# A fused transformer block: softplus on VectorE, the scan's operands in four tiles of their own, its temporaries in the residual's tiles

## The chip, the core and the metric

The kernel runs on one core of a Trainium2 chip. The metric is device microseconds of one execution, the median over runs. TensorE (PE) is shown in two rows of the profile, PE for matmuls and PEld for weight loads; VectorE is DVE, ScalarE is ACT, GpSimd is POOL, and SP is the queue that issues all DMAs. Instructions of an engine run in the order in which they stand in its program, and an instruction that waits holds up everything behind it on that engine.

## What is computed

Two transformer blocks follow each other on 512 tokens of width 1024. The change lies in the first, in the state-space branch beside the banded attention. Per token and head a step size is made from a narrow projection; it scales a causal decay, and a chunked scan (four chunks of 128 tokens here, two groups of eight heads) carries a state from chunk to chunk:

```python
dt = jax.nn.softplus(dt_raw + dt_bias)
A = -jnp.exp(a_log)
X = x * dt[..., None];  a = dt * A
decay_in = jnp.exp(where(tril, a_cum[l] - a_cum[s], -inf))
y_diag = (C B^T * decay_in) X          # per chunk
states = B^T (exp(a_cum[-1] - a_cum) * X)
y_off  = C prev * exp(a_cum)           # prev: state carried so far
h = h + concat(att, gated ssd) @ w_out
```

The residual `h` is first needed where the output projection of the first block is added to it.

## The kernel before

All dense products run as three fp32r matmuls each (high and low halves, lines 167 to 175), in units of 24 matmuls of 128x512 for each 512 KB of weights. A unit is loaded by SP (line 137), its high half is made by ACT (line 156, tile wh) and its low half by DVE or POOL (line 157, tile wl). Three raw buffers and two of each half rotate; the split of a unit runs one unit ahead of its use.

The order of the matmuls on PE is the order of the code. The other engines' instructions are placed by a scheduler that works from its own timeline, by priority; inside `tc.high_priority()` an instruction is placed before others that could run. The dense stream is a generator that yields after every 12 matmuls; such a stretch is called a tick here. `drive` (line 221) lets the side work advance at each tick: a `yield True` of a side generator ends its turn for that tick, so what follows it in the code comes at least one tick of dense matmuls later on PE. In the first dense stage (`dense1`, lines 794 to 798) one side moves per tick, in the second (`dense1z`) two.

The side work that matters:

- `norm_side` (466): sums of squares for the first norm. In line 472 it also starts the eight loads of the residual, 256 KB each, into the tiles `h`, which until then held the transposed input; SP issues them in the first 30 us, and nothing reads them before the output projection.
- `conv` (481): of each finished row of 128 channels a depthwise convolution: line 483 takes the row out of PSUM into `u`, ACT scales it (485), three DVE steps add the shifted copies (487), ACT takes a tanh (490), DVE finishes (491). It runs on every unit of the first dense stage, so DVE is busy with it while the step size is made.
- `dt_side` (496): the narrow projection, then the softplus as a series. Lines 511 to 521 are on DVE and ACT, lines 522 to 533 are 21 instructions on POOL, on tiles of 128x64 (one of 128x16), each waiting for the one before. The last ones make `da` (the decay exponent, line 531) and its high and low parts `dah` and `dal`. Eight ticks later PE sums `da` over the tokens (lines 537 to 539), ACT takes the exponential `ex` (540).
- `am_pair` (565): for half the heads of one scan step, ACT writes eight 128x128 blocks, the lower-triangle mask scaled by `dah` and `dal`, into two tiles. They come from the shared arena RA, of which 16 tiles are free then, so ACT can write them several steps ahead.
- `ssd_side` (573): the scan, eight steps, first the four chunks of group 0, then those of group 1. At the head of a step PE makes C B^T (591) and the segment sums of both halves (604, 605; they read the four `am` tiles), ACT takes the exponentials (608), DVE multiplies by the masked C B^T (609). One tick later (two in the first two steps) PE multiplies the result with X (622, 16 small matmuls), the carried state (629) and makes the new state (636). X, Xd, M and t are temporaries of the arena FA.
- `val_evac` (651): at the end of the last unit of `dense1`, ACT takes four banks of values out of PSUM (line 654). The next dense matmul (the first row of q) goes to the first of these banks.

Temporaries, attention and gating share FA, 28 tiles.

Of the kernel before, what the change touches and what calls it, by code (L numbers as in the profile page):

```python
# [9 lines left out]
F32 = mybir.dt.float32  # L10
F32R = mybir.dt.float32r
I32 = mybir.dt.int32
AF = mybir.ActivationFunctionType
ALU = mybir.AluOpType
# [59 lines left out]
class Both:  # L74
# [11 lines left out]
    def room(self, n):  # L86
        return len(self.own.free_list) + len(self.shared.free_list) >= n


@with_exitstack  # L90
def mixer_kernel(ctx, tc, xT, xN, wst, wfa, wfb, wdt, wgrp, rbt, par, con, frow, out):
# [313 lines left out]
    with ExitStack() as ph:  # L405
# [4 lines left out]
        RB = Both(Arena(fa_p, 5, F32R, "fx"), RA)  # L410
        lw = {}
# [54 lines left out]
        def norm_side():  # L466
            for _ in range(4):
                yield True
            ssb = col_sums(acc)
            FA.put(acc)  # L470
            for k in range(KD):
                nc.sync.dma_start(out=h[k], in_=xN[(k // 2) * 128:(k // 2 + 1) * 128, (k % 2) * 512:(k % 2 + 1) * 512])
            rsqrt(rcol1, ssb[:, 0:NT], NT, 1.0 / D, 1e-5)
            V.tensor_scalar(out=rhalf1, in0=rcol1, scalar1=0.5, scalar2=None, op0=ALU.mult)
            dg = bcast_diag(rcol1, FA)
            yield True
            yield True
            lw["rb1"] = bcast_rows(dg, FA)
            yield True
# [16 lines left out]
        def dt_side():  # L496
# [12 lines left out]
            with tc.high_priority():  # L509
# [12 lines left out]
                G.tensor_tensor(out=dz, in0=dz, in1=du, op=ALU.mult)  # L522
                G.tensor_tensor(out=dz2, in0=dz, in1=dz, op=ALU.mult)
                G.tensor_scalar(out=dp, in0=dz2, scalar1=2.0 / 15, scalar2=2.0 / 13, op0=ALU.mult, op1=ALU.add)
                for n in (11, 9, 7, 5, 3, 1):
                    G.tensor_tensor(out=dp, in0=dp, in1=dz2, op=ALU.mult)
                    G.tensor_scalar(out=dp, in0=dp, scalar1=2.0 / n, scalar2=1.0, op0=ALU.add, op1=ALU.mult)
                G.tensor_tensor(out=dp, in0=dp, in1=dz, op=ALU.mult)
                G.tensor_tensor(out=dt, in0=dx, in1=dp, op=ALU.add)
                G.tensor_scalar(out=aexp, in0=aexp, scalar1=-1.0, scalar2=1.0, op0=ALU.mult, op1=ALU.mult)  # L530
                G.tensor_tensor(out=v3(da), in0=v3(dt), in1=bc_mid(aexp, NT), op=ALU.mult)
                G.tensor_copy(out=dah, in_=da)
                G.tensor_tensor(out=dal, in0=da, in1=dah.bitcast(F32), op=ALU.subtract)
# [29 lines left out]
        prev = {}  # L563

        def am_pair(c, g, q):
            o = c * 16 + g * 8 + q * 4
            amh, aml = RA.take(2)
            for t, a in ((amh, dah.bitcast(F32)), (aml, dal)):
                for j in range(4):
                    S.activation(out=col(t, j), in_=C("le"), func=AF.Copy, scale=a[:, o + j:o + j + 1])  # L570
            return amh, aml

        def ssd_side():
# [3 lines left out]
            am = [am_pair(0, 0, 0), am_pair(0, 0, 1)]  # L577
            yield False
            for n, (c, g) in enumerate(seq):
# [8 lines left out]
                X = FA.get()  # L588
# [7 lines left out]
                if c < NT - 1:  # L596
                    Xd = FA.get()
# [4 lines left out]
                for q in range(2):  # L602
# [3 lines left out]
                    RA.put(*am[q])  # L606
                    M = FA.get()
# [3 lines left out]
                if n + 1 < len(seq):  # L611
                    c1, g1 = seq[n + 1]
                    am = [am_pair(c1, g1, 0), am_pair(c1, g1, 1)]
                G.tensor_tensor(out=h8(xt), in0=h8(xt), in1=bc_in(P("d_skip")[:, g * 8:g * 8 + 8], 64), op=ALU.mult)
                yield True
                if n < 2:
                    yield True
# [6 lines left out]
                FA.put(*Ms)  # L624
                FA.put(X)
                V.tensor_tensor(out=xt, in0=xt, in1=yb, op=ALU.add)
                if c > 0:
                    ob = ax_bank()
                    PE.matmul(ob, lhsT=col(CT, c), rhs=prev[g], start=True, stop=True)
                    t = FA.get()  # L630
                    V.tensor_tensor(out=h8(t), in0=h8(ob), in1=hs(ex[:, 0:64], c, g), op=ALU.mult)
                    G.tensor_tensor(out=xt, in0=xt, in1=t, op=ALU.add)
                    FA.put(t)
                if c < NT - 1:
                    nb = ax_bank()
                    PE.matmul(nb, lhsT=bt, rhs=Xd, start=True, stop=True)
                    FA.put(Xd)
# [9 lines left out]
                yield True  # L647

# [112 lines left out]
        def z_evac(g):  # L761
            def f(c, b):
                y = xs_tok[c, g]
# [738 lines left out]
```

## Time and profile before

| what | value |
|---|---|
| time, median of 3 runs | 1442.28 us (1441.97 to 1442.55) |
| the profiled execution | 1444.04 us, of it 1442.3 us of span, 1.7 us around it |
| mean granted TensorE clock | 0.998 |
| busy: PE, DVE, ACT, POOL | 1421.2, 1006.5, 695.8, 235.7 us |
| the change's stage | about 40 to 240 us of the span |

How to read the profile's rows: a row of the timeline has the start in us, the time in us, engine, line, operation, tiles (out<-in) and a count where several are merged; in square brackets stands how long the engine was idle before it and what ended the wait. Rows of several instructions overlap at the ends, because an instruction's start can lie before the end of the one ahead: what an instruction costs its engine is the distance from its start to the next start. Rows of the windows give, for each stretch, the busy time of each engine, then the granted clock (PEclk, 1.00 is full speed).

### The profile page before, as it was taken

How to read it: one execution, taken by the hardware profiler on the slowest of the kernel's cores; microseconds unless marked ns; L12 is line 12 of the kernel's file. 1: busy time of each engine (PE TensorE's matmuls, PEld its weight loads, DVE VectorE, ACT ScalarE, POOL GpSimd, SP SyncE). 2: the span in 40 equal slices, each digit the busy share in tenths (PEclk: the TensorE clock that was granted, in tenths of full speed). 3: DMA queues.
4: the chain of work that ended last, by engine and by line, in shares of the span. 5: the costliest groups of instructions: out<-in, count | busy, mean ns of one | idle time of the engine just before them, and what ended most of it. 6: DMA issues, size and time to landing. Idle time of an engine off the chain costs nothing.

```text
span 1442.3 us, 18031 instructions
## 1 busy us (share of the span) xinstructions
PE 1421.2 (99%) x6683; PEld 1172.9 (81%) x6683; DVE 1006.5 (70%) x1763; ACT 695.8 (48%) x1236; POOL 235.7 (16%) x220
## 2 busy tenths in 40 slices
PE   8999999999999999999999999999999999999998
PEld 5777888888888888888878888888888888888887
DVE  7774565655977778677774666777645977878676
ACT  5584645424544435345444646464324544545453
POOL 4322520000010010102262433221110010010101
PEclk9999999999999999999999999999999999999999
DMA  7221532223533241420233433342233433141411
GB/s 256 60 87 54 138 98 81 71 88 112 180 96 114 65 149 44 161 74 30 95 92 96 125 95 99 103 116 68 88 102 126 167 103 117 59 146 45 161 30 59
DMA packets 46408, 145.91 MB, mean 101 GB/s; under 512 B 5872, under 2 KB 6128, under 8 KB 46320
## 3 DMA queue, kind: packets, MB, share of 16 engines
q1 hardware_dynamic: 46320, 144.76, 32.4%
q8 instruction: 52, 0.85, 0.3%
q14 instruction: 36, 0.29, 0.1%
HBM read 131.63 MB, written 2.10 MB: 93 GB/s over the span
## 4 chain that ended last, share of the span: by engine, by line
PE 83%; DVE 9%; POOL 2%; ACT 2%; issue 2%; DMA 1%; SPq 0%; POOLq 0%; ACTq 0%; DVEq 0%
PE mm L170 13%; PE mm L168 13%; PE mm L169 13%; PE mm L173 10%; PE mm L174 10%; PE mm L175 10%; DVE wl L157 2%; PE ax L174 2%; PE ax L173 2%; PE ax L175 2%; DVE s L1258 1%; PE ax L728 1%; PE ax L1270 1%; PE ax L384 1%; PE ax L622 1%
## 5 line engine op out<-in xcount | busy, mean ns | idle before, releaser
L168 PE MATMUL mm<-r,wh 128*128 128x512 f32 x928 | 368.2, 397 | 3.0 <-ACT wh L156 2.9
L170 PE MATMUL mm<-r,wl 128*128 128x512 f32 x928 | 362.4, 391 | 1.5 <-DVE wl L157 1.5
L169 PE MATMUL mm<-r,wh 128*128 128x512 f32 x928 | 362.3, 390 | 1.4 <-DVE r L294 1.0
L156 ACT ACTIVATE wh<-wr 128x1024 fp32r<-128x1024 f32 (+1 forms) x173 | 182.4, 1054 | 369.3 <-PE mm L169 151.0
L157 DVE TENSOR_TENSOR wl<-wr,wh 128x1024 fp32r<-128x1024 f32 (+1 forms) x171 | 230.3, 1347 | 118.0 <-ACT wh L156 117.4
L168 PEld LDWEIGHTS mm<-r,wh 128*128 128x128 f32 x928 | 174.7, 188 | 40.8 <-ACT wh L156 3.3
L169 PEld LDWEIGHTS mm<-r,wh 128*128 128x128 f32 x928 | 174.6, 188 | 39.3 <-DVE r L294 2.0
L173 PE MATMUL mm<-wh,r 128*128 128x512 f32 x512 | 206.3, 403 | 0.0
L170 PEld LDWEIGHTS mm<-r,wl 128*128 128x128 f32 x928 | 174.6, 188 | 39.0 <-DVE wl L157 2.5
L174 PE MATMUL mm<-wl,r 128*128 128x512 f32 x512 | 199.7, 390 | 0.3 <-DVE wl L157 0.3
L175 PE MATMUL mm<-wh,r 128*128 128x512 f32 x512 | 199.8, 390 | 0.0
L299 POOL TENSOR_TENSOR vl<-u,vh 128x512 fp32r<-128x512 f32 x36 | 48.2, 1350 | 751.0 <-ACT vh L298 682.7
L174 PEld LDWEIGHTS mm<-wl,r 128*128 128x128 f32 x512 | 96.4, 188 | 21.6 <-issue 2.2
L173 PEld LDWEIGHTS mm<-wh,r 128*128 128x128 f32 x512 | 96.4, 188 | 21.2 <-issue 2.2
L175 PEld LDWEIGHTS mm<-wh,r 128*128 128x128 f32 x512 | 96.1, 188 | 20.4
L298 ACT ACTIVATE vh<-u 128x512 fp32r<-128x512 f32 x100 | 63.0, 631 | 50.7 <-PE mm L175 36.5
L938 DVE TENSOR_TENSOR h<-h,mm 128x512 f32<-128x512 f32 x80 | 52.4, 679 | 19.7 <-PE mm L175 19.7
L353 ACT ACTIVATE s<-s,nm 128x128 f32<-128x128 f32 (+1 forms) x96 | 52.6, 550 | 19.1 <-DVE nm L350 19.1
L298 ACT ACTIVATE wh<-u 128x1024 fp32r<-128x1024 f32 (+1 forms) x32 | 32.3, 1009 | 61.2 <-PE mm L175 61.2
L298 ACT ACTIVATE wh<-t 128x1024 fp32r<-128x1024 f32 x32 | 34.0, 1063 | 56.1 <-PE mm L169 32.5
L299 DVE TENSOR_TENSOR wl<-u,wh 128x1024 fp32r<-128x1024 f32 (+1 forms) x32 | 38.0, 1188 | 24.7 <-ACT wh L298 24.7
L299 DVE TENSOR_TENSOR vl<-u,vh 128x512 fp32r<-128x512 f32 x64 | 43.7, 682 | 0.0
(342 smaller groups left out, 2335.2 us busy)
## 6 DMA issues: line engine op xcount, KB each, us to landing
wr<-in_wst_dram SPq DMA_DIRECT2D x171, 512.0 KB, 3.6
u<-in_wfa_dram SPq DMA_DIRECT2D x32, 512.0 KB, 4.6
u<-in_wfb_dram SPq DMA_DIRECT2D x32, 512.0 KB, 4.4
r<-r SPq DMA_DIRECT2D x56, 128.0 KB, 2.8
h<-in_xT_dram SPq DMA_DIRECT2D x8, 256.0 KB, 6.3
h<-in_xN_dram SPq DMA_DIRECT2D x8, 256.0 KB, 4.7
f<-in_rbt_dram SPq DMA_DIRECT2D x8, 256.0 KB, 2.9
gr<-gr SPq DMA_DIRECT2D x16, 128.0 KB, 2.7
```

Of the source, the lines that this page charges most:

```text
L156: S.activation(out=hi[:, p], in_=t[:, p], func=AF.Copy)
L157: eng.tensor_tensor(out=lo[:, p], in0=t[:, p], in1=hi.bitcast(F32)[:, p], op=ALU.subtract)
L168: PE.matmul(ps, lhsT=wh, rhs=xh, start=first, stop=False)
L169: PE.matmul(ps, lhsT=wh, rhs=xl, start=False, stop=False)
L170: PE.matmul(ps, lhsT=wl, rhs=xh, start=False, stop=last)
L173: PE.matmul(ps, lhsT=xh, rhs=wh, start=first, stop=False, **kw)
L174: PE.matmul(ps, lhsT=xh, rhs=wl, start=False, stop=False, **kw)
L175: PE.matmul(ps, lhsT=xl, rhs=wh, start=False, stop=last, **kw)
L298: S.activation(out=hi, in_=src, func=AF.Copy)
L299: (eng or V).tensor_tensor(out=lo, in0=src, in1=hi.bitcast(F32), op=ALU.subtract)
L353: S.activation(out=s[:, SOFF[i]:SOFF[i] + n], in_=s[:, SOFF[i]:SOFF[i] + n], func=AF.Exp, bias=nm[:, i:i + 1], accum_out=Z[:, i:i + 1])
L938: V.tensor_tensor(out=ht(c, g), in0=ht(c, g), in1=b, op=ALU.add)
```

## The change

Five things are done, in the first block alone.

1. The softplus series moves from POOL to DVE: the 21 instructions there become 15 on DVE, since the multiply by the square and the addition of the next coefficient now go in one step. They stay inside `tc.high_priority()`.
2. `am_pair` takes its tiles from a new arena AM of four tiles. Four is what one scan step holds, so the tiles of the next step are written only after PE has read those of the present one.
3. The scan's steps are spread: the two halves of the next step's operands are written on two ticks, so that each step has two ticks between its head and its products with X (before: two in the first two steps, one in the others), and the first step starts one tick later.
4. X, Xd, M and t live in the eight tiles `h`. The loads of the residual move from `norm_side` to the end of `ssd_side`.
5. An assertion at the gate's evacuation, without an instruction.

```diff
+class Loan(Arena):
+    def __init__(self, tiles):
+        self.free_list = list(tiles)
+        self.low = len(tiles)
...
+        AM = Arena(fa_p, 4, F32R, "fm")
...
-            for k in range(KD):
-                nc.sync.dma_start(out=h[k], in_=xN[(k // 2) * 128:(k // 2 + 1) * 128, (k % 2) * 512:(k % 2 + 1) * 512])
             rsqrt(rcol1, ssb[:, 0:NT], NT, 1.0 / D, 1e-5)
...
-                G.tensor_tensor(out=dz, in0=dz, in1=du, op=ALU.mult)
-                G.tensor_tensor(out=dz2, in0=dz, in1=dz, op=ALU.mult)
-                G.tensor_scalar(out=dp, in0=dz2, scalar1=2.0 / 15, scalar2=2.0 / 13, op0=ALU.mult, op1=ALU.add)
-                for n in (11, 9, 7, 5, 3, 1):
-                    G.tensor_tensor(out=dp, in0=dp, in1=dz2, op=ALU.mult)
-                    G.tensor_scalar(out=dp, in0=dp, scalar1=2.0 / n, scalar2=1.0, op0=ALU.add, op1=ALU.mult)
-                G.tensor_tensor(out=dp, in0=dp, in1=dz, op=ALU.mult)
-                G.tensor_tensor(out=dt, in0=dx, in1=dp, op=ALU.add)
-                G.tensor_scalar(out=aexp, in0=aexp, scalar1=-1.0, scalar2=1.0, op0=ALU.mult, op1=ALU.mult)
-                G.tensor_tensor(out=v3(da), in0=v3(dt), in1=bc_mid(aexp, NT), op=ALU.mult)
-                G.tensor_copy(out=dah, in_=da)
-                G.tensor_tensor(out=dal, in0=da, in1=dah.bitcast(F32), op=ALU.subtract)
+                V.tensor_tensor(out=dz, in0=dz, in1=du, op=ALU.mult)
+                V.tensor_tensor(out=dz2, in0=dz, in1=dz, op=ALU.mult)
+                V.tensor_scalar(out=dp, in0=dz2, scalar1=2.0 / 15, scalar2=None, op0=ALU.mult)
+                for n in (13, 11, 9, 7, 5, 3):
+                    V.scalar_tensor_tensor(out=dp, in0=dp, scalar=2.0 / n, in1=dz2, op0=ALU.add, op1=ALU.mult)
+                V.scalar_tensor_tensor(out=dp, in0=dp, scalar=2.0, in1=dz, op0=ALU.add, op1=ALU.mult)
+                V.tensor_tensor(out=dt, in0=dx, in1=dp, op=ALU.add)
+                V.tensor_scalar(out=aexp, in0=aexp, scalar1=-1.0, scalar2=None, op0=ALU.mult)
+                V.tensor_tensor(out=v3(da), in0=v3(dt), in1=bc_mid(aexp, NT), op=ALU.mult)
+                V.tensor_copy(out=dah, in_=da)
+                V.tensor_tensor(out=dal, in0=da, in1=dah.bitcast(F32), op=ALU.subtract)
...
+        FB = Loan(h)
 
         def am_pair(c, g, q):
             o = c * 16 + g * 8 + q * 4
-            amh, aml = RA.take(2)
+            amh, aml = AM.take(2)
...
-            am = [am_pair(0, 0, 0), am_pair(0, 0, 1)]
-            yield False
+            am = []
+            for q in range(2):
+                am.append(am_pair(0, 0, q))
+                yield True
...
-                X = FA.get()
+                X = FB.get()
...
-                    RA.put(*am[q])
-                    M = FA.get()
+                    AM.put(*am[q])
+                    M = FB.get()
...
-                if n + 1 < len(seq):
-                    c1, g1 = seq[n + 1]
-                    am = [am_pair(c1, g1, 0), am_pair(c1, g1, 1)]
                 G.tensor_tensor(out=h8(xt), in0=h8(xt), in1=bc_in(P("d_skip")[:, g * 8:g * 8 + 8], 64), op=ALU.mult)
-                yield True
-                if n < 2:
+                am = []
+                for q in range(2):
+                    if n + 1 < len(seq):
+                        am.append(am_pair(*seq[n + 1], q))
                     yield True
                 yb = ax_bank()
...
                 yield True
+            for k in range(KD):
+                nc.sync.dma_start(out=h[k], in_=xN[(k // 2) * 128:(k // 2 + 1) * 128, (k % 2) * 512:(k % 2 + 1) * 512])
```

The line numbers of the changed kernel are higher by 4 to 8 in this part: 483, 487, 491 become 488, 492, 496; 531 becomes 535; 541 becomes 545; 570 becomes 575; 608 becomes 615; 622 becomes 628; 654 becomes 662.

The scheduler places the instructions of DVE and ACT anew. On DVE, before, this stood where the last pieces of the convolution of row 3 (tile f_164) are added up; the series is on POOL, and the only trace of it here is `dtdo` (dt is its result, ex the exponential of the sums):

```order
L541 TENSOR_TENSOR dtdo<-dt,ex 128x64
L487 SCALAR_TENSOR_TENSOR f_164<-u_260,cw,f_164 128x512
L157 TENSOR_TENSOR wl<-wr,wh 128x1024
L483 TENSOR_TENSOR u_260<-mm,rb 128x512
L487 SCALAR_TENSOR_TENSOR f_166<-u_259,cw,f_166 128x512 x3
L491 SCALAR_TENSOR_TENSOR f_164<-f_165,f_164 128x512
```

Now the end of the series stands there, the rest of it one by one between the convolution's steps ahead of this place (dp is the series' value, dz_254 the square):

```order
L492 SCALAR_TENSOR_TENSOR f_164<-u_264,cw,f_164 128x512
L531 SCALAR_TENSOR_TENSOR dp<-dp,dz_254 128x64
L532 SCALAR_TENSOR_TENSOR dp<-dp,dz 128x64
L533 TENSOR_TENSOR dt<-dx,dp 128x64
L496 SCALAR_TENSOR_TENSOR f_164<-f_165,f_164 128x512
L535 TENSOR_TENSOR da<-dt,aexp 128x64
L536 CAST dah<-da 128x64
L537 TENSOR_TENSOR dal<-da,dah 128x64
L545 TENSOR_TENSOR dtdo<-dt,ex 128x64
```

So `da` now comes behind the last step of the convolution of row 3, which itself waits for ACT's tanh f_165. Ahead of this place, from the moment PE has finished row 3 (u_264 is read out of PSUM), DVE has in this order: line 488, 492, 496, one step of the series, the low half of a unit (line 163), 492 twice, a step of the series, 492, 496, a step of the series, and then the rows shown.

On ACT, in the third scan step (chunk 2 of group 0), before, this was the end of the step's work: the second exponential (line 608), the rest of the operands two steps later (tiles r_118, r_119), and then the four values (line 654):

```order
L608 ACTIVATE f_160<-ax 128x512
L570 ACTIVATE r_118<-con,dah 128x128 x2
L570 ACTIVATE r_119<-con,dal 128x128 x4
L654 ACTIVATE f_164<-mm,rcol_127 128x512
L654 ACTIVATE f_156<-mm,rcol_127 128x512
L654 ACTIVATE f_157<-mm,rcol_127 128x512
L654 ACTIVATE f_152<-mm,rcol_127 128x512
```

Now the same instructions stand in nearly the same order (fm_175 and fm_176 are the third and fourth of the four tiles):

```order
L615 ACTIVATE h_89<-ax 128x512
L575 ACTIVATE fm_175<-con,dah 128x128 x2
L575 ACTIVATE fm_176<-con,dal 128x128 x2
L662 ACTIVATE f_154<-mm,rcol_127 128x512
L575 ACTIVATE fm_176<-con,dal 128x128
L662 ACTIVATE f_156<-mm,rcol_127 128x512
```

What moved is not visible on ACT but on PE: this scan step's head now stands one tick later there, 12 matmuls before the end of the last value unit; before, it stood 24 ahead of it.

On SP the eight loads of the residual now stand, four and four, around one weight load, behind the last scan step, which in PE's order comes after 636 dense matmuls (the last scan step came after 552 before); the output projection begins after 768.

More of the change, by code (lines that the diff above doesn't have):

```diff
@@ L596, in ssd_side @@
                 if c < NT - 1:
-                    Xd = FA.get()
+                    Xd = FB.get()
                     G.tensor_tensor(out=h8(Xd), in0=h8(xt), in1=hs(dtdo, c, g), op=ALU.mult)
@@ L623, in ssd_side @@
                                   start=True, stop=True)
-                FA.put(*Ms)
-                FA.put(X)
+                FB.put(*Ms)
+                FB.put(X)
                 V.tensor_tensor(out=xt, in0=xt, in1=yb, op=ALU.add)
@@ L629, in ssd_side @@
                     PE.matmul(ob, lhsT=col(CT, c), rhs=prev[g], start=True, stop=True)
-                    t = FA.get()
+                    t = FB.get()
                     V.tensor_tensor(out=h8(t), in0=h8(ob), in1=hs(ex[:, 0:64], c, g), op=ALU.mult)
                     G.tensor_tensor(out=xt, in0=xt, in1=t, op=ALU.add)
-                    FA.put(t)
+                    FB.put(t)
                 if c < NT - 1:
@@ L636, in ssd_side @@
                     PE.matmul(nb, lhsT=bt, rhs=Xd, start=True, stop=True)
-                    FA.put(Xd)
+                    FB.put(Xd)
                     if c == 0:
@@ L762, in f @@
             def f(c, b):
+                assert ("ssd", g) in ready
                 y = xs_tok[c, g]
```

## The prediction

> **What bounds the kernel now.** I read the page first, then PE's timeline for its gaps, then what ended each gap.
>
> ```profile
> span 1442.3 us, 18031 instructions
> PE 1421.2 (99%) x6683; PEld 1172.9 (81%) x6683; DVE 1006.5 (70%) x1763; ACT 695.8 (48%) x1236; POOL 235.7 (16%) x220
> ```
>
> PE is busy for all but 21 us, and the change takes no matmul away. So it can only win gaps of PE, and the time that the clock is lowered behind a gap. PE's timeline in the change's stage (each row with the gap ahead of it):
>
> ```profile
> 63.17 0.33 PE L537 MATMUL ax<-da,con 128*128 128x64 f32 x2
> ...
> 66.13 0.39 PE L169 MATMUL mm<-r,wh 128*128 128x512 f32 x1
> 66.36 0.39 PE L170 MATMUL mm<-r,wl 128*128 128x512 f32 x1
> 69.62 0.50 PE L168 MATMUL mm<-r,wh 128*128 128x512 f32 x1 [2.88 <-ACT wh L156]
> ...
> 70.88 0.79 PE L170 MATMUL mm<-r,wl 128*128 128x512 f32 x1 [0.38 <-DVE wl L157]
> ```
> ```profile
> 91.62 0.50 PE L604 MATMUL ax<-r,gt_r 128*128 128x512 f32 x1 [0.79 <-ACT f L555]
> ...
> 100.42 1.67 PE L622 MATMUL ax<-f,f 128*128 128x64 f32 x8 [1.79 <-DVE f L609]
> ```
> ```profile
> 119.70 0.38 PE L591 MATMUL ax<-f,f 128*128 128x128 f32 x2
> ...
> 119.95 0.48 PE L604 MATMUL ax<-r,gt_r 128*128 128x512 f32 x1
> ...
> 120.97 0.39 PE L173 MATMUL mm<-wh,r 128*128 128x512 f32 x1
> ...
> 123.70 1.00 PE L622 MATMUL ax<-f,f 128*128 128x64 f32 x8
> 125.84 1.10 PE L622 MATMUL ax<-f,f 128*128 128x64 f32 x8 [1.14 <-DVE f L609]
> ```
>
> A dense matmul costs 66.36 - 66.13 = 0.23 us, a tick of twelve 123.70 - 120.97 = 2.73 us. Five gaps lie here. The first comes from the softplus: ACT's operands for the scan (line 570) stand in ACT's program ahead of a unit's high half (line 156), and they wait for POOL's series.
>
> ```profile
> 62.15 2.16 ACT L570 ACTIVATE r<-con,dah 128x128 fp32r<-128x128 f32 x7 [4.88 <-POOL dah L532]
> ...
> 68.53 1.04 ACT L156 ACTIVATE wh<-wr 128x1024 fp32r<-128x1024 f32 x1
> ```
> ```profile
> 49.70 0.58 POOL L522 TENSOR_TENSOR dz<-dz,du 128x64 f32<-128x64 f32 x1 [23.30 <-DVE dz L521]
> ...
> 61.15 0.33 POOL L531 TENSOR_TENSOR da<-dt,aexp 128x64 f32<-128x64 f32 x1
> 61.53 0.58 POOL L532 CAST dah<-da 128x64 fp32r<-128x64 f32 x1
> ```
>
> POOL takes from 49.70 to 61.48 for `da`. PE wants it at 63.17 and has it; only ACT is late. The granted clock shows what a gap costs behind itself:
>
> ```profile
> 70.00:74.00 4.00, 3.62 (x10) 2.53 (x9) 4.00 (x7) 4.00 (x13) 0.00 (x0) 0.57 0.43 131
> 100.00:104.00 4.00, 3.58 (x11) 2.55 (x12) 2.77 (x5) 1.86 (x5) 0.00 (x0) 0.60 0.00 0
> 124.00:128.00 4.00, 2.86 (x18) 2.13 (x17) 1.48 (x3) 2.81 (x9) 0.06 (x1) 1.00 0.28 112
> ```
>
> Behind the gap of 2.88 us the clock is 0.57 over 4 us, behind that of 1.79 it is 0.60, behind 1.14 it stays at 1.00. A lowered stretch loses up to 0.43 x 4 = 1.7 and 0.40 x 4 = 1.6 us.
>
> **The change part by part.**
>
> *What goes, 10.4 us.* With the operands written step by step, no operand waits ahead of the high half any more: the gap at 69.62 goes (69.62 - 66.36 - 0.23 = 3.0 us), the one at 70.88 (0.4) and the clock behind them (1.7): 5.1 us. With two ticks between a step's head and its products everywhere and with the scan one tick later, the gaps at 91.62 (0.8), 100.42 (1.8 and 1.6 of clock) and 125.84 (1.1) go: 5.3 us. What is late next there: the second half of M. In the old third step the second exponential starts at 124.48, 4.8 us behind the step's head at 119.70, and M is done 1.4 us later (125.84); with two ticks PE wants it at 1.27 + 2 x 2.73 + 0.45 = 7.2 us. One us of cover is left, so I put these at nothing.
>
> *The series on DVE, 7.5 us of new loss.* DVE's rows give the price of each kind of step between starts:
>
> ```profile
> 43.30 0.22 DVE L514 TENSOR_TENSOR dx<-dx,dz 128x64 f32<-128x64 f32 x1
> 43.43 1.41 DVE L487 SCALAR_TENSOR_TENSOR f<-u,cw,f 128x512 f32<-128x512 f32 x2
> 44.76 0.22 DVE L515 TENSOR_TENSOR dx<-dx,par 128x64 f32<-128x64 f32 x1
> 45.24 1.23 DVE L157 TENSOR_TENSOR wl<-wr,wh 128x1024 fp32r<-128x1024 f32 x1 [0.26 <-ACT wh L156]
> 46.38 1.41 DVE L487 SCALAR_TENSOR_TENSOR f<-u,cw,f 128x512 f32<-128x512 f32 x2
> ...
> 47.81 0.69 DVE L483 TENSOR_TENSOR u<-mm,rb 128x512 f32<-128x512 f32 x1
> 48.41 0.68 DVE L491 SCALAR_TENSOR_TENSOR f<-f,f 128x512 f32<-128x512 f32 x1
> 49.01 0.55 DVE L521 RECIPROCAL dz<-dz 128x64 f32<-128x64 f32 x1
> ...
> 60.64 0.69 DVE L483 TENSOR_TENSOR u<-mm,rb 128x512 f32<-128x512 f32 x1 [0.49 <-PE mm L170]
> ```
>
> A small step costs 43.43 - 43.30 = 0.13 us, or its whole 0.22 when the next one needs it; a convolution step 0.66 (44.76 - 43.43, halved), a low half 1.14, lines 483 and 491 0.60 each. In the series the arithmetic is short: 15 x 0.2 = 3 us against POOL's 12. But DVE's program puts the convolution between its steps. The row at 60.64 waits for PE alone, so it stands there in the changed kernel too. From it, in the changed order: 483 0.60, 487 0.66, 491 0.60, series 0.13, low half 1.14, 487 twice 1.32, series 0.13, 487 0.66, 491 0.60, series 0.13, 487 0.66: 67.27. Then two series steps, their last product and the sum, 0.8: 68.1, where ACT's tanh for line 491 is ready too (it follows the step that ends at 67.35, 0.6 us long). Line 491 0.60 and `da` 0.22: 68.9 us. PE wants `da` at 63.17 with the same matmuls ahead of it. So PE waits 5.8 us at line 537, and the whole dense stream is queued behind. No low half is late by it: the ones between come ahead of the units that need them. If the series were done as early as DVE could, the wait is zero; that is the other end. I take 5.8, since each step of the sum is a row and DVE takes its program in order.
>
> Behind a gap of 5.8 us the clock is low when PE starts again. The two lowered stretches above cost 1.6 and 1.7; part of this one lies in the gap, but a second may follow: 0.9 to 2.6, I take 1.7. Sum 7.5 us.
>
> Two waits follow from it, which I put at nothing. On ACT the sixteen first operands come behind `da`, some 0.3 us each by the last row of ACT's further below, so until about 74 us; `ex` and the high half of a unit stand behind them, until about 75, and PE wants that half only a unit of 24 matmuls (5.5 us) after it has restarted and finished its present one, near 79. On DVE `dtdo` waits for `ex`, and line 483 of the next row behind it; PE finishes that row near 74 itself. Cost without this cover: the rest of the four or five us.
>
> *Four tiles, 4.0 us of new loss.* The first operand of the next step now waits on ACT until PE has read the present one's, and behind it on ACT stand the exponentials, the high halves and the four values (line 654). Third step, whose head now lies 12 matmuls before the end of the value unit:
>
> ```profile
> 120.92 0.97 ACT L570 ACTIVATE r<-con,dah 128x128 fp32r<-128x128 f32 x3
> ...
> 124.48 0.58 ACT L608 ACTIVATE f<-ax 128x512 f32<-128x512 f32 x1
> ...
> 125.54 1.27 ACT L570 ACTIVATE r<-con,dal 128x128 fp32r<-128x128 f32 x4
> 129.45 2.76 ACT L654 ACTIVATE f<-mm,rcol 128x512 f32<-128x512 f32 x4 [2.63 <-PE mm L175]
> ```
>
> These are the same instructions as in the changed order. From the first operand to the middle of the last four (line 654 now comes after two of them) they take 125.54 + 0.59 - 120.92 = 5.2 us. They can start when PE has ended line 604, 119.95 + 0.48 - 119.70 = 0.7 us behind the head, so the first value is out at 0.7 + 5.2 + 2.76 / 4 = 6.6 us. PE wants its bank at 123.70 - 119.70 = 4.0 us behind the head, for the first row of q. So PE waits 2.6 us. The clock behind it: nothing (as behind 1.14) to 1.6 (as behind 1.79), I take 1.3. Sum 3.9, rounded to 4.0. If the two operand rows were not ahead of it, nothing: that is the other end.
>
> Here a page of the Trainium skill can be weighed. "TensorE: Matmul & The Clock Gate", Part 1 (The HAM clock gate), says that the clock is halved after at least one idle window of about 3.4 us, and that the windows run free of the kernel. The rows differ from that rule taken at its word: gaps of 2.88 and 1.79 us were enough. By the rule the gap of 5.8 us lowers the clock too, and that of 2.6 does not: the sum would be 1.3 us lower. The sum above goes by the rows.
>
> *The residual's loads, nothing.* They leave SP's program in the first 30 us, where no gap of PE is put down to a DMA; the longest there:
>
> ```profile
> PE mm L170 <- DVE wl L157: 1.1, 1, 1.1
> PE mm L169 <- DVE r L294: 1.0, 1, 1.0
> ```
>
> At the new place they wait for the last scan step, and one weight load waits behind the first four of them.
>
> ```profile
> 220.80 18.41 SPq L137 DMA_DIRECT2D wr<-in_wst_dram  x3
> ```
> ```profile
> h<-in_xN_dram SPq DMA_DIRECT2D x8, 256.0 KB, 4.7
> ```
>
> Three weight loads go out in 18 us there, each as soon as one of three buffers is free, two units ahead of its use: a delay of some us is covered. The residual is needed 132 matmuls later, over 30 us at 0.23 each, against 4.7 us of landing. Cost if the cover were gone: one landing, 5 us. POOL, freed of 12 us of series, is not on the path.
>
> **The sum.** 1444.04 for the profiled execution, less 10.4, plus 7.5, plus 4.0: 1445.1, that is +1.1 us. The profiled execution lies 1.8 above the median of 1442.28, which I take as the same for both kernels: 1443.4 us.
>
> **The rivals.**
>
> 1. The series keeps up with PE (DVE's waits elsewhere leave it room): the 7.5 go, 1443.4 - 7.5 = 1435.9. For it: the arithmetic is 3 us. Against it: the order and the row at 60.64. 0.06.
> 2. The value banks are not late (ACT starts the third step's operands far enough ahead of PE): the 4.0 go, 1439.4 or a little less. For it: PE comes later to this place by the first wait, and ACT may gain on it. Against it: the operands wait for PE's own read, so ACT cannot run ahead. 0.15.
> 3. The other side: the operands, now written only just before use, make M late as before. Place: line 622 of the first three steps; price: the 5.3 us stay, 1448.7; it decides as soon as ACT has over 1 us of other work (a high half is 1.04) between the operands and the second exponential. 0.12.
> 4. The group 1 steps, moved from beside q and k into the attention's stage, add gaps of 1 us each at three or four of them: 1446 to 1447. For it: DVE puts two products with the step size ahead of the negated maximum there. Against it: no such gap of over 0.5 us now. 0.13.
>
> **How the numbers follow.** The forecast has what is left, 0.54, and its own range is 1440.5 to 1446 by the bounds above. A measurement of this kernel tells about 0.2%, 2.9 us, from no change. Faster by more than that: rival 1 and most of rival 2, 0.20. Slower: rivals 3 and 4, 0.25. Same: 0.55. The range takes in rival 2 and rival 4 and reaches towards 3: 1438.5 to 1447.5.
>
> **What would show it.** Right: PE's row at line 541 with a wait of 5 to 6 us for DVE's `da` near 69 us; a PE row of the first q matmul with 2 to 3 us waiting for ACT's value (line 662) near 127 us; no wait at line 628 in group 0; clock near 0.6 behind both gaps. Wrong: `da` done by 64 us; operands of the third step on ACT that do not wait for PE; a wait for a DMA at the output projection; any gap over 1 us from 150 to 240.

## The result, and the profile after

The changed kernel takes 1452.36 us (median of 4 runs, 1452.00 to 1453.00) against 1442.41 us of the kernel before (1441.97 to 1444.92). The ratio, an estimate from all runs and not the quotient of the two medians, is 1.0066, with a 95% interval of 1.0048 to 1.0083. Forecast were 1443.4 us, with a range to 1447.5. The change costs 10 us where the forecast had one, and the result lies above its range. The profiled execution took 1452.30 us.

Page of the changed kernel, the span and the engines' rows:

```profile
span 1450.5 us, 18032 instructions
PE 1423.7 (98%) x6683; PEld 1174.3 (81%) x6683; DVE 1008.3 (70%) x1778; ACT 696.3 (48%) x1236; POOL 223.5 (15%) x199
```

PE does the same matmuls and sits idle for 5.7 us more. PE's waits of the changed kernel, grouped (us in total, times, longest):

```profile
PE ax L541 <- DVE da L535: 5.7, 1, 5.7
PE mm L174 <- ACT f L662: 2.6, 1, 2.6
...
PE ax L611 <- ACT f L404: 2.3, 2, 1.6
...
PE ax L400 <- ACT s L359: 0.8, 3, 0.4
```

Lines 541 and 174 are the two waits that the prediction named, with the sizes that it gave. Lines 611 and 400 are new, and no term of the sum had them. PE's timeline of the changed kernel at these places:

```profile
62.75 0.39 PE L176 MATMUL mm<-r,wl 128*128 128x512 f32 x1
68.87 0.66 PE L541 MATMUL ax<-da,con 128*128 128x64 f32 x2 [5.73 <-DVE da L535]
...
127.36 0.79 PE L174 MATMUL mm<-r,wh 128*128 128x512 f32 x1 [2.62 <-ACT f L662]
...
149.32 0.39 PE L174 MATMUL mm<-r,wh 128*128 128x512 f32 x1
...
166.69 0.27 PE L400 MATMUL ax<-con,s 128*128 128x128 f32 x1
167.11 0.33 PE L400 MATMUL ax<-con,s 128*128 128x128 f32 x1 [0.15 <-ACT s L359]
...
168.41 1.29 PE L400 MATMUL ax<-con,s 128*128 128x128 f32 x7 [0.38 <-ACT s L359]
...
170.13 0.27 PE L600 MATMUL ax<-con,f 128*128 128x128 f32 x1
172.01 0.79 PE L611 MATMUL ax<-fm,gt_r 128*128 128x512 f32 x1 [1.61 <-ACT f L404]
...
208.77 0.49 PE L598 MATMUL ax<-f,f 128*128 128x128 f32 x2 [0.29 <-DVE f L406]
209.10 0.27 PE L600 MATMUL ax<-con,f 128*128 128x128 f32 x1
210.04 0.50 PE L611 MATMUL ax<-fm,gt_r 128*128 128x512 f32 x1 [0.67 <-ACT f L404]
...
253.88 0.48 PE L179 MATMUL mm<-wh,r 128*128 128x512 f32 x1
```

The rows at 149.32 and 253.88 are marks: the 442nd and the 673rd matmul into `mm`. At the first, group 0's scan is done and group 1's not begun in either kernel; at the second all of the scan is done. In the kernel before the same two start here:

```profile
148.11 0.39 PE L168 MATMUL mm<-r,wh 128*128 128x512 f32 x1
...
246.09 0.48 PE L173 MATMUL mm<-wh,r 128*128 128x512 f32 x1
```

So the changed kernel is 149.32 - 148.11 = 1.2 us late when group 0 is done, and 253.88 - 246.09 = 7.8 us late when group 1 is: 6.6 us are lost between. Up to the first mark the forecast of +1.1 came true; behind it I had forecast nothing. From the 673rd matmul on the difference stays the same to 0.2 us until the last matmul. From the forecast of 1443.4 us to the measured 1452.36 are 9.0 us: 6.6 are lost in group 1, 1.8 are a step from the profiled execution to the median that should not have been taken (further below), and the small rest is spread.

The granted clock over the four us behind the three long waits (the column behind POOL's):

```profile
68.87:72.87 4.00, 4.00 (x13) 3.47 (x14) 0.31 (x2) 3.88 (x14) 0.00 (x0) 0.55 0.00 0
127.36:131.36 4.00, 4.00 (x11) 3.19 (x12) 0.77 (x1) 3.20 (x6) 0.00 (x0) 0.60 0.00 0
172.00:176.00 4.00, 3.99 (x12) 3.20 (x13) 0.75 (x2) 3.29 (x12) 0.65 (x1) 0.64 0.64 199
```

By the missing share of the clock they lose 0.45 x 4 = 1.8, 1.6 and 1.4 us on top of the waits.

What holds the bank of line 611? ACT's timeline of the changed kernel there, and DVE's and POOL's ahead of the late exponentials (line 359):

```profile
166.07 0.40 ACT L359 ACTIVATE s<-s,nm 128x128 f32<-128x128 f32 x1 [4.55 <-DVE nm L356]
...
169.22 1.05 ACT L162 ACTIVATE wh<-wr 128x1024 fp32r<-128x1024 f32 x1
170.17 0.62 ACT L364 ACTIVATE r<-f 128x512 fp32r<-128x512 f32 x1
170.81 0.63 ACT L365 ACTIVATE r<-f 64x512 fp32r<-64x512 f32 x1
171.46 0.66 ACT L404 ACTIVATE f<-ax 128x384 f32<-128x384 f32 x2
```
```profile
159.99 2.21 DVE L163 TENSOR_TENSOR wl<-wr,wh 128x1024 fp32r<-128x1024 f32 x1
...
162.74 2.37 DVE L596 TENSOR_TENSOR h<-f,dt 128x512 f32<-128x512 f32 x2
165.03 1.01 DVE L356 TENSOR_SCALAR nm<-mx 128x4 f32<-128x4 f32 x1
...
179.97 0.17 DVE L356 TENSOR_SCALAR nm<-mx 128x4 f32<-128x4 f32 x1
```
```profile
159.84 1.29 POOL L376 TENSOR_TENSOR r<-f,r 128x512 fp32r<-128x512 f32 x1 [3.63 <-ACT r L374]
161.11 3.44 POOL L605 TENSOR_TENSOR h<-f,dtdo 128x512 f32<-128x512 f32 x2
164.52 2.50 POOL L618 TENSOR_TENSOR f<-f,par 128x512 f32<-128x512 f32 x2
```

The matmuls outside the dense stream share a ring of four PSUM banks (`ps_ax`). An attention head (its scores, their softmax, the products with the values) transposes its scores into all four (line 400), and DVE and ACT copy these out in turn (lines 406 and 404). The head of a scan step, that is its first matmuls (lines 598 to 612), follows in the same tick and wants three banks. The second of these, at line 611, is the one whose copy stands on ACT behind a high half (line 162) and two splits (lines 364 and 365), until 171.46 + 0.5 = 172.0. The exponentials of this attention head are late too, since the products with the step size (line 596) stand ahead of the negated maximum (line 356) on DVE. These two products take 2.37 us beside POOL's; the shortest of the eight in this kernel takes 0.68.

### The profile page after: what moved, and what is told of

It is laid out like the page before. It is cut to its first block, busy times and chain, and to the rows that moved or that the text cites. A ratio compares the mean times of both kernels' runs of the same rounds, so it can differ in the third digit from the quotient of the medians.

```text
span 1450.5 us, 18032 instructions
## 1 busy us (share of the span) xinstructions
PE 1423.7 (98%) x6683; PEld 1174.3 (81%) x6683; DVE 1008.3 (70%) x1778; ACT 696.3 (48%) x1236; POOL 223.5 (15%) x199
## 4 chain that ended last, share of the span: by engine, by line
PE 78%; DVE 7%; issue 2%; ACT 2%; POOL 2%; DMA 1%; SPq 0%; POOLq 0%; ACTq 0%
PE mm L174 12%; PE mm L175 12%; PE mm L176 12%; PE mm L179 10%; PE mm L180 10%; PE mm L181 10%; PE ax L180 2%; PE ax L179 2%; PE ax L181 2%; DVE wl L163 2%; DVE s L1267 1%; PE ax L736 1%; PE ax L390 1%; PE ax L1279 1%; PE ax L392 1%
```

## The experiments

**Theory.** The terms of the prediction hold (the wait for `da`, the wait for the values), and group 1 adds 6.6 us because of its phase, the place of its steps within the attention's round. A step now lasts three ticks, and so does an attention head (one tick each for its scores, the products of the attention head before with the values, and its transposes). So the head of each step in group 1 comes behind an attention head's transposes: after 504, 540, 576 and 612 dense matmuls. In the kernel before, steps of two ticks came after 468, 492, 516 and 540, and moved through the phases; only the last met the transposes, and it did not wait. **Rivals**: the steps lose beside the attention whatever their phase; or DVE, with the series on it, is what limits the whole stage.

The changed kernel is compared with the four runs above, all others with the kernel before on the same chip (medians of 1443.2 to 1443.5 us over 12 to 16 runs). The intervals of two rows together leave about 3 us open where their ratios are compared. "Group 0" and "group 1" are what a run loses (or wins) against the kernel before up to the first mark and from there to the second, in its profiled execution, taken like the marks above, less the difference of 0.0 to 0.9 us that is there ahead of the change (at the 181st dense matmul). "-" stands where the scan is not at the same place at the first mark. These two columns are of one execution each, which lies up to 2 us below its median (B, D) or up to 2.7 above it (E).

| kernel | ratio, 95% interval | group 0, us | group 1, us |
|---|---|---|---|
| changed kernel | 1.0066, 1.0048 to 1.0083 | +1.4 | +6.6 |
| A series on POOL | 1.0026, 1.0016 to 1.0037 | -3.4 | +6.5 |
| B second tick in group 0 alone | 1.0072, 1.0056 to 1.0089 | +1.3 | +6.6 |
| C group 1 two ticks later | 1.0035, 1.0022 to 1.0048 | +1.9 | +2.2 |
| D values on DVE | 1.0038, 1.0023 to 1.0052 | -1.7 | +5.2 |
| E sums over `da` two ticks later | 1.0040, 1.0025 to 1.0055 | +0.6 | +6.9 |
| F all of the scan two ticks later | 0.9983, 0.9973 to 0.9992 | - | - |
| G as C, ahead of the transposes | 1.0032, 1.0021 to 1.0044 | +1.5 | +1.6 |
| H old ticks | 1.0046, 1.0029 to 1.0062 | +0.3 | +6.8 |
| I copies on DVE | 1.0076, 1.0061 to 1.0092 | +2.7 | +8.1 |
| J kernel before, series on DVE | 1.0022, 1.0013 to 1.0031 | +2.8 | 0.0 |
| K series on POOL, scan two ticks later | 0.9971, 0.9959 to 0.9982 | - | - |
| L as K, copies on DVE | 0.9961, 0.9948 to 0.9973 | - | - |

**A. Series on POOL** (lines 527 to 537 as in the kernel before).

```diff
-                V.tensor_tensor(out=dz, in0=dz, in1=du, op=ALU.mult)
+                G.tensor_tensor(out=dz, in0=dz, in1=du, op=ALU.mult)
...
```

> The changed kernel with its softplus series put back on POOL as before; the extra tick, the four operand tiles and the lent tiles stay. Sum theory (the three stretches of PE's waits add up: da 5.7 us of wait and about 1.8 of lowered clock, first q row 2.6 and 1.6, group 1 beside the attention some 6.5): the wait at line 541 goes, the others stay, 1452.4 - 7.5 = about 1445 us. Rival, DVE limits this stage whatever is on it: PE's head start is lost again in waits for DVE behind it, 1450 or more. Both: no row of PE waits for da; POOL has da near 61.5 us.

1447.0 us: 0.0040 less than the changed kernel, 5.8 us. Between the two profiled executions, 4.8 us of it come ahead of the first mark and 0.1 from there to the second. So the series is a cost of group 0 alone, and the rival falls: PE's head start is not lost again. It is less than 7.5 because an old gap comes back. PE's timeline of A:

```profile
68.48 0.50 PE L174 MATMUL mm<-r,wh 128*128 128x512 f32 x1 [1.71 <-ACT wh L162]
```

ACT still writes the first operands as soon as POOL has `dah`, ahead of the high half. Writing them in two ticks did not part them from it; in the changed kernel the gap is only covered by the longer wait for `da`.

**B. The second tick in group 0 alone.**

```diff
-                    yield True
+                    if q == 0 or n < 4:
+                        yield True
```

> The changed kernel with the second tick between a step's head and its products only in the first four steps (group 0); the steps of group 1 have one, as before. Phase theory (a step of three ticks beside an attention head of three ticks puts every head of group 1 behind the attention's four transposes, where the head needs their banks): only two of the four heads still come there, so most of 6.5 us goes, 1446 to 1448 us. Rival (the steps cost PE their waits beside the attention whatever their phase, since DVE and ACT have too much there): 1451 to 1453 us, with the waits at other lines.

1453.7 us: no gain, and group 1 loses the same 6.6. The expectation failed, though not for the rival's reason. Heads now come at 504, 528, 552 and 576; of these 504 and 576 still stand behind transposes, and those are the two of the four that cost. Line 611 waits at 171.57 us for the same 1.61 us as in the changed kernel, and at 214.68 for 0.74.

I had counted all four as equal. In the changed kernel the second head (its line 611 at 190.51 us) waits for nothing: ACT has no high half and no split ahead of the copy then. The third head has them again; ACT's timeline of the changed kernel:

```profile
207.25 1.06 ACT L162 ACTIVATE wh<-wr 128x1024 fp32r<-128x1024 f32 x1 [5.78 <-issue]
```

The counts suggest why. A unit of weights lasts 24 matmuls, two ticks, and near the start of each, ACT makes the high half of a following one: here at 169.22, 182.38, 196.92, 207.25 and 219.08 us. 504 and 576 are whole units, 540 and 612 lie in the middle of one. So the first and the third head meet the making of a half, the second and the fourth do not.

**C. Group 1 two ticks later**, so that its heads come with the products with the values.

```diff
                     yield from xs_side(g)
+                if n == 4:
+                    for _ in range(2):
+                        yield True
```

> The changed kernel with two more ticks ahead of the first step of group 1, three ticks a step as before: every head of group 1 then comes with the attention's products with the values (one bank) and every step's products with the scores. Phase theory: the waits at the transposes and at line 611 for ACT's copies go, 1446 to 1447 us. Rival (too much work beside the attention whatever the phase): 1451 to 1454 us.

1448.6 us, 0.0031 (4.5 us) less than the changed kernel, if more than the 1446 to 1447 expected, and group 1 loses 2.2 us in place of 6.6. Same steps, same three ticks, the same engines: the phase makes two thirds of the loss. The rest is the late exponentials (1.4 us, unchanged) and 0.8 us at line 390 for a copy of ACT's, which stands behind sixteen operands, a high half and two splits.

**G. The same two ticks ahead of group 1's token transposes.**

```diff
-                    for _ in range(3):
+                    for _ in range(3 if g == 0 else 5):
                         yield True
                     yield from xs_side(g)
```

> The changed kernel with two more ticks ahead of group 1's token transposes (not behind them): heads as in the run with two ticks behind them, and the step-size products of the first two tokens come behind the first head's negated maximum on DVE and beside less of POOL's work. If those products are what makes the first scores late (1.4 us at the transposes of line 400), that goes too and the ratio is about 1.0025 against 1.0035 of that run. Rival (the low half of 2.2 us beside POOL's split of k makes them late): no change, 1.0035.

1448.1 us, the same as C within the intervals. The products do stand behind the negated maximum now and the exponentials are in time, but the wait has only moved: the transposes that turn group 1's rows into tokens (line 557) meet the banks of the same attention transposes. DVE's and PE's timeline of G:

```profile
162.88 0.17 DVE L356 TENSOR_SCALAR nm<-mx 128x4 f32<-128x4 f32 x1
```
```profile
168.06 0.66 PE L557 MATMUL ax<-con,f 128*128 128x128 f32 x4 [0.59 <-ACT f L404]
```

**I. Copies on DVE**, for the first four attention heads.

```diff
-            if (j + flip) % 2:
+            if (j + flip) % 2 and not dve:
...
-            at[hh] = (probs_T(s, FA, hh), rz)
+            at[hh] = (probs_T(s, FA, hh, hh < 4), rz)
```

> The changed kernel with the copies of the first four attention heads' transposed scores (line 406) all on DVE, where before every second one was on ACT; the scan stays where it is. Bank theory: line 611 waits for a bank that ACT's copy frees late, since a high half and two splits stand ahead of it on ACT; with DVE's copies the waits of 1.85 and 0.92 us and the 1.5 us of clock behind the first go, about 4 us: a ratio of 1.0038 against 1.0066 of the changed kernel. Rival (four copies and a low half in a row make DVE as late): 1.006 or more.

1454.7 us: the rival was right. Line 611 now waits for DVE's copy, which stands behind a low half. At the first head the wait is shorter than ACT's was (0.92 us against 1.61) and the clock stays up. At the third head it is longer (1.68 against 0.67), and the clock is granted 0.57 over the next four us. Timeline of I, PE and DVE:

```profile
172.83 0.50 PE L611 MATMUL ax<-fm,gt_r 128*128 128x512 f32 x1 [0.92 <-DVE f L406]
...
211.16 0.73 PE L611 MATMUL ax<-fm,gt_r 128*128 128x512 f32 x1 [1.68 <-DVE f L406]
```
```profile
171.22 1.23 DVE L163 TENSOR_TENSOR wl<-wr,wh 128x1024 fp32r<-128x1024 f32 x1
172.36 0.61 DVE L406 COPY f<-ax 128x256 f32<-128x256 f32 x2
```

So ACT by itself is not the cause. A step's head right behind four transposes waits for whichever engine empties the banks, when that engine has a unit's half to make; C changes that, I does not. It is the first and the third head again, with the copies all on the other engine.

**D. Values on DVE.**

```diff
-                S.activation(out=t, in_=b, func=AF.Copy, scale=rcol1[:, c:c + 1])
+                V.tensor_scalar(out=t, in0=b, scalar1=rcol1[:, c:c + 1], scalar2=None, op0=ALU.mult)
```

> The changed kernel with the four values taken out of their banks by DVE instead of ACT; nothing else changed. Sum theory: the first q row waits no more for ACT, which has sixteen operands ahead of the values; 2.6 us of wait and 1.6 of lowered clock go, 1452.4 - 4.2 = 1448.2 us. Rival (another wait takes its place at once, the third step's products at line 628 or DVE's low halves): 1451 to 1453 us.

1449.1 us: 0.0028 or 4.0 us less than the changed kernel, against 4.2 expected and 4.0 in the prediction. No wait for a value is left. In the profiled execution, 4.4 us are won between the 217th and the 397th dense matmul, around the place of this wait. It differs from the changed kernel's at two other places too, where the waits are the same and only the clock is not. D's windows there (the clock is the column behind POOL's), and PE's row at the start of the second:

```profile
72.20:76.20 4.00, 4.00 (x14) 3.17 (x13) 1.43 (x3) 2.72 (x7) 0.00 (x0) 0.69 0.00 0
168.30:172.30 4.00, 4.00 (x19) 3.37 (x20) 0.74 (x2) 3.58 (x13) 0.65 (x1) 1.00 0.66 200
```
```profile
168.30 0.50 PE L611 MATMUL ax<-fm,gt_r 128*128 128x512 f32 x1 [1.62 <-ACT f L404]
```

Behind the wait of 5.73 us for `da` the clock stays low longer than in the changed kernel, which has 1.00 from 72.87 to 76.87: 1.2 us more. Behind the wait at line 611 it is not lowered at all. That is why group 1 loses 5.2 us here and not 6.6: the difference is the clock's 1.4.

**E. The sums over `da` two ticks later**, the rest of the scan where it was.

```diff
-            for _ in range(8):
+            for _ in range(10):
                 yield True
             cum = ax_bank()
...
                 am.append(am_pair(0, 0, q))
-                yield True
```

> The changed kernel with the three sums over da asked for two ticks later; the two ticks behind the first operands are dropped, so that every step of the scan stays at its place among the dense matmuls. Sum theory: PE wants da at 62.75 + 2 x 2.73 = 68.2 us and has it at 68.7, so 0.5 us of the wait of 5.7 is left and no lowered clock behind it: 7 us less than the changed kernel, a ratio to the kernel before of about 1.0018. Rival (the first operands, ex and dtdo now come too late for the first step, or DVE is the limit here): a new wait at the first head or its products, 1.004 or more.

1448.9 us, 0.0026 (3.8 us) less and not 7. PE asks 5.2 us later, at 67.94 + 0.23, but `da` comes later too, and the wait shrinks by 2.1 us only; what more the ratio shows lies within the intervals. PE's and DVE's timeline of E:

```profile
71.96 0.41 PE L541 MATMUL ax<-da,con 128*128 128x64 f32 x2 [3.63 <-DVE da L535]
```
```profile
67.47 1.22 DVE L163 TENSOR_TENSOR wl<-wr,wh 128x1024 fp32r<-128x1024 f32 x1
68.60 0.22 DVE L531 SCALAR_TENSOR_TENSOR dp<-dp,dz 128x64 f32<-128x64 f32 x1
...
71.60 0.22 DVE L535 TENSOR_TENSOR da<-dt,aexp 128x64 f32<-128x64 f32 x1
```

Another row's convolution and low half now stand between the steps of the series: PE gets on and feeds DVE more work, and the order puts it ahead of the series. The series has no place of its own in DVE's program.

**F. All of the scan two ticks later** (E's first edit alone).

> The changed kernel with the three sums over da and all of the scan two ticks later. Sum theory: 7 us less by da; the heads of group 1 come with the attention's products with the values, as in the run that put only group 1 two ticks later, 4.3 us less; the second step's operands now stand a whole unit ahead of the first q row, so that its wait of 2.6 us and the clock behind it shrink too, by 0 to 4.2: a ratio to the kernel before between 0.9960 and 0.9988. Rival (a scan that comes later loses at its end what it wins at its start): 1.001 or more, with waits of z's rows for the scan.

1440.6 us, faster than the kernel before by 0.17%. Three things come with one number: `da` (a wait of 3.6 us is left), the phase of group 1 as in C, and the values. The last shows on ACT's timeline of F:

```profile
118.44 2.39 ACT L662 ACTIVATE f<-mm,rcol 128x512 f32<-128x512 f32 x4
...
125.23 0.99 ACT L575 ACTIVATE fm<-con,dah 128x128 fp32r<-128x128 f32 x3 [3.46 <-PE ax L611]
```

The values leave their banks 6.8 us ahead of the third step's operands, and PE does not wait.

**H. Old ticks**, two only in the first two steps.

```diff
-                    yield True
+                    if q == 0 or n < 2:
+                        yield True
```

> The changed kernel with the old rule for ticks (two between head and products in the first two steps, one in the others); series on DVE, four tiles and lent tiles stay, the scan still one tick later than before. Theory: the heads of group 1 come at 480, 504, 528 and 552 dense matmuls as against 504, 540, 576 and 612; only the second comes with the attention's transposes, so about 4 us of 6.5 go, and the late M of the third and fourth step (1 us each at line 628) come back: a ratio of about 1.0050. Rival (as with one tick in group 1 alone, it makes no difference when the steps come): 1.0070.

1450.7 us, near the 1.0050 expected, by other terms than expected. Group 0 loses only 0.3 although M (the product of exponentials and mask, line 616) is late again in its third and fourth step, since the wait for the values is gone. Group 1 still loses 6.8, now by a late M, a late copy of ACT's (`bt`, line 607) and a low clock behind them (0.50 over the four us behind the second row). PE's timeline of H:

```profile
166.46 1.16 PE L629 MATMUL ax<-h,h 128*128 128x64 f32 x8 [0.81 <-DVE h L616]
169.33 2.04 PE L643 MATMUL ax<-h,bt 128*128 128x512 f32 x2 [1.71 <-ACT bt L607]
```

With one tick, the first products of group 1 come while ACT has operands ahead of M's exponentials, and operands and the attention's exponentials ahead of `bt`. So another phase alone did not help here. Whether the second tick is worth having at a better phase is not shown, since no run with the four tiles has one tick there.

**J. The kernel before with the series on DVE** (the series as in the changed kernel).

```diff
-                G.tensor_tensor(out=dz, in0=dz, in1=du, op=ALU.mult)
+                V.tensor_tensor(out=dz, in0=dz, in1=du, op=ALU.mult)
...
```

> The kernel before with its softplus series on DVE, nothing else changed. Theory: DVE's walk is the same as in the changed kernel, so da comes near 68.7 us and PE waits 5.8 us with some 1.8 us of clock behind it; ACT's operands stand behind da and behind the high half, so that the gap of 3.0 us at line 156 and its clock go (5.1 us): +2.5 us, a ratio of 1.0017. If the high half stays late as well: +7.5, 1.0052. Rival (DVE alone is no loss): 1.000 or less.

1446.9 us, 3.2 us more than the kernel before by the ratio (2.5 expected). The series by itself makes the same wait; PE's waits of J:

```profile
PE ax L536 <- DVE da L530: 5.7, 1, 5.7
```

The gap at the high half goes under it, as in the changed kernel, and group 1 loses nothing (0.0): the loss there is not the series'.

**K and L. The edits together**: series on POOL and the scan two ticks later (K), with I's copies on DVE (L).

> The changed kernel with the series back on POOL and the sums over da and all of the scan two ticks later. Sum theory: against the run with the series on POOL alone (1.0026) the phase in group 1 saves 4.3 us and the first q row's wait with its clock 4.2, as each did by itself: a ratio of 0.9967. Rival (the three savings share one cover): 0.998 or more.

> The same as the run with the series on POOL and the scan two ticks later, and the copies of the first four attention heads' transposed scores on DVE. Bank theory: the waits of 0.6 to 1.0 us that are left behind those transposes for ACT's copies go too, 1 to 2 us: a ratio of 0.9955 to 0.9960. Rival: DVE's copies are no earlier, 0.9967.

1438.75 and 1437.26 us: 0.29% and 0.39% faster than the kernel before, the fastest of the study, and close to what the sums gave. Whether I's copies help here, where no head stands behind the transposes, the intervals don't settle. The longest wait that is left in L is 2.4 us for the high half at line 162, the gap that A shows.

## Why the prediction was wrong, point by point

*The series on DVE.* Right. The walk along DVE's program gave 68.9 us for `da`; DVE's timeline of the changed kernel:

```profile
60.46 0.69 DVE L488 TENSOR_TENSOR u<-mm,rb 128x512 f32<-128x512 f32 x1 [1.15 <-PE mm L176]
...
68.51 0.22 DVE L535 TENSOR_TENSOR da<-dt,aexp 128x64 f32<-128x64 f32 x1
```

`da` is there at 68.73 and PE waits 5.73 us (5.8 forecast), with 1.8 us of clock (1.7). The wait is the walk's merit; that the clock agrees to 0.1 us is luck, since behind the same wait D's execution lost 1.2 us more. E shows the limit of such a walk: it holds for one order, and an edit elsewhere gives another.

*The four tiles.* Right: a wait of 2.6 us at the first q row (2.6 forecast), 1.6 of clock (1.3). The first value was forecast 6.6 us behind the third step's head, which is at 120.59 us; it comes at 127.2. ACT's timeline of the changed kernel:

```profile
121.41 0.99 ACT L575 ACTIVATE fm<-con,dah 128x128 fp32r<-128x128 f32 x3 [5.75 <-PE ax L611]
...
126.63 0.68 ACT L662 ACTIVATE f<-mm,rcol 128x512 f32<-128x512 f32 x1
```

D bears the price out: 4.0 us by the ratio, with some 3 us of room, and 4.4 at the place itself.

*What goes.* The gaps at the scan (5.3 us) went: no product of group 0 waits for M. The one at the high half went for another reason than I gave (A). In the sum it made no difference, because the wait for `da` covers it.

*The residual's loads, `ex`, the high half behind the operands, `dtdo`: nothing.* Right; no wait of PE above 0.3 us is for any of them, and none for a DMA.

*The extra tick in group 1.* Here it failed. The sum has no term for it. "What is late next there" was answered with M alone, for group 0's steps, and the attention came up only in the fourth rival, at 0.13: "the group 1 steps, moved from beside q and k into the attention's stage, add gaps of 1 us each at three or four of them". Place and sign were right and half of the mechanism (two products ahead of the negated maximum); a gap of over 1 us from 150 to 240, which the prediction named as a sign of being wrong, stands at 172.01. But 6.6 us were lost and not 3 or 4, and what the fourth rival lacked was the bank: a step's head that wants banks which the attention's transposes have just filled. Two heads, not four, made the loss, and one of the waits also lowered the clock. I had walked group 0 instruction by instruction and given group 1 a sentence. The tick counts of both generators were at hand: three and three never drift apart. From the rows at 166.69 to 210.04: late exponentials 168.41 - 166.69 less three transposes of 0.12, 1.4; line 611 first time 172.01 - 170.13, 1.9; clock 1.4; at the third head waits of 0.3 and 210.04 - 209.10, 1.2. That makes 5.9 of the 6.6.

*From the profile to the median.* I took 1.8 us off, as the profiled execution lay that far above three runs. In three later sets of runs of the kernel before, 43 in all, the medians were 1443.2 to 1443.5, so the profiled one (1444.04) was 0.5 to 0.8 above them. The changed kernel's profiled execution (1452.30) is at its median (1452.36): the step took 1.8 us off a forecast that needed none.

*The clock.* The Trainium skill's page "TensorE: Matmul & The Clock Gate", Part 1 (The HAM clock gate), taken at its word would have spared the clock behind the wait of 2.62 us; the row grants 0.60 there, and 0.64 behind 1.61. The rows were the better guide.

What stays open: why the first and third head cost and not the second and fourth is read from the counts and from ACT's and DVE's programs; B and I agree, but were not made for it. The share of the four operand tiles in group 1 is not tested, since no run gives the old tiles back; in C and H, ACT's operands stand ahead of the late copies. And 0.7 of the 6.6 us are not accounted for.

## What to carry to other kernels

When an edit changes how many ticks a piece of work takes, write down the period of what it runs beside: equal periods lock, and a bad meeting then comes back. Here it came back in every second round, because a third period, the unit's two ticks, had a part in it. Walk every stage that the edit reaches with the same care, above all the one to which work is moved. And a chain of small steps on a busy in-order engine is not worth its arithmetic but the work that stands between its steps.

## What the runs showed of the hardware

The clock was lowered behind a wait of 1.61 us (0.64 over 4 us, changed kernel at 172.0) and not behind one of 1.71 (A at 68.48, where no 2 us of its trace from 60 to 100 us show less than full clock), nor in D behind a wait of 1.62 at the same place in the program (1.00 over 4 us from 168.30). In J it was lowered behind 1.17 us (0.68 over 4 us from 102.94) and not behind 1.18 (1.00 from 94.75). So the length of a wait of this size does not settle it. The times go with the clock in part: 43 runs of the kernel before lie between 1441.8 and 1445.8 us, those with a mean clock of 0.999 between 1441.9 and 1442.3, and the longest has 0.996.

Beside POOL's products some of DVE's steps took twice their time and more: a low half 2.21 us against 1.22, a negated maximum of 128x4 elements 1.01 us against 0.17. The Trainium skill's page "SBUF — State Buffer", section "SBUF: two separate sides", says that the two engines share a pair of ports as a lock, for some kinds of DVE's instructions, and that the loser is blocked for the other's whole instruction. The rows agree: the negated maximum starts at 165.03 beside two products of POOL's that take 2.50 us together from 164.52 on, and ends at 166.04, after about one of them. In G, POOL is idle from 161.15 to 166.92, and there the same negated maximum takes 0.17 us. At one place where DVE was first it did not slow: the changed kernel's low half at 170.30 took 1.22 us, and it was POOL's product, started at 170.87 beside it, that took 1.78 us where its like at 159.84 took 1.29. That the ports are the cause, no run here shows.
